# An MLP of split float32 products: matmuls in written order, weights two items ahead, sums given out by quota

## The chip, the cores and the metric

One core of one Trainium2 chip runs the whole kernel. The metric is the device time of one execution in microseconds (us), the median of several runs.

## The reference

One layer of a hybrid encoder on 256 positions (SEQ) of width 2048 (D), in float32. Ahead of the MLP stand one projection, two kinds of attention, a recurrent mixer and an output projection; the change does not touch them. The MLP is the last line:

```
D_MODEL, SEQ, D_FF = 2048, 256, 4 * 2048

def _rms_norm(x, gain):
    y = x * lax.rsqrt(jnp.mean(x * x, axis=-1, keepdims=True) + RMS_EPS)
    return y * gain

hdn = jnp.square(jax.nn.relu(_rms_norm(x, norm_mlp_pre) @ w_mlp_up))    # 256 x 8192
x = x + _rms_norm(hdn @ w_mlp_down, norm_mlp_post)                      # 256 x 2048
```

## The kernel before, in words

**A float32 product as three.** Each float32 operand is split in two parts, hi and lo, that TensorE (PE) multiplies in its faster float32 form; hi x hi, hi x lo and lo x hi are added up in PSUM. Weights come from DRAM in pieces of 128 x 1024 (512 KB) on SyncE's (SP's) DMA queue, three buffers `raw` for the up weights (L136) and six, `raw2`, for the down weights (L963). `wsplit` (L140) makes of a piece `whi`, a copy on ScalarE (ACT, L144), and `wlo`, a subtraction on VectorE (DVE, L145), three buffers of each. Activations lie as hi and lo beside each other in tiles `pk` (128 x 512).

**Entry of the MLP.** The residual `x1` is finished piece by piece on DVE (`add_mixed`, L878), turned by PE (L907, into PSUM buffers of the pool `mps`), and split into the 16 tiles `upk2` on ACT (L225) and DVE (L226). The up matmuls need these tiles one after the other.

**Items.** From there the work is a list of items, each with a `prep`, which asks for a weight piece and splits it, and a `run`, which issues the matmuls. `drive` (L939) takes them one after the other. Ahead of an item's `run` it calls the `prep` of this one and of the next one (`AHEAD` is 1), so far as that is not done. What a `run` leaves behind it goes to the list `posts` and is called right behind the next item's `run`.

- `up(q, j)` (L978) is one hidden column, 128 of the 8192 hidden units: two items of half a column. Each is one `gemm` over 8 tiles: 8 matmuls of 128 x 512 and 8 of 128 x 256 (L160, L164, L166). The column's sum lies in one of the four buffers of the PSUM pool `gps`. Its post is the evacuation: ACT copies the second half to `tmp` (L991), DVE adds the first (L992), ACT takes ReLU (L993) and square (L997).
- `forms(q, m)` (L1011) makes of two columns the seven left factors of a Strassen-like product (7 products of blocks in place of 8): sums `sfm` on DVE (L1015 to L1017), hi on ACT, lo on DVE (to L1022).
- `down(q, sb)` (L1025) is one group: the products F1 to F7 for a quarter q of the hidden units and half sb of the output columns, in four steps d. An item is one product in one step: its `prep` makes the right factor out of raw pieces, with an addition on DVE (L1033) or a DMA that accumulates (issued by GpSimd, POOL, L1036), and splits it; its `run` is 6 matmuls (L1069 to L1071). F3, F7 and F1 gather in three buffers of `gps`, F6, F2, F5 and F4 in the four of `mps`. Behind the last step (d = 3) stand the sums of the seven products into the output `y`: on DVE (L1076) and, for first ones, on ACT (L1081, L1093).

**Order of the work.** The first `drive` runs 16 columns of `up(0, ...)` with their forms. The second runs 6 groups (q = 0 to 2, sb = 0 and 1) of 4 iterations (d), 24 in all. An iteration's list (L1145) is F3, the two halves of column ua, a form, F7, F1 among them, then F6, F2, the first half of column ub, a form, F5, the second half, F4; ua and ub are the next quarter's columns. Behind the second `drive`, `tok` (L204) computes the last quarter's down product without the seven forms.

The program is written in the order of these calls. On each engine a scheduler of the framework then sets the final order, and is free to put an instruction ahead of others that were written before it. Inside `tc.manual_schedule` the engines that are named there keep the written order; an earlier stage of the kernel does this for PE (L747), the MLP does not.

Of the kernel before, what the change touches and what calls it, by code (L numbers as in the profile page):

```python
# [12 lines left out]
AF = mybir.ActivationFunctionType  # L13
ALU = mybir.AluOpType
# [6 lines left out]
AHEAD = 1  # L21
# [28 lines left out]
def hybrid_block(ctx, tc, xt, x, gains, params, consts, lora, gup, wst, out):  # L50
# [80 lines left out]
    wq = []  # L131
    side = []

    def wraw(n=None):
        raw = wpool.tile([128, HALF], F32, tag="raw", name=nm("raw"), bufs=3)
        nc.sync.dma_start(out=raw, in_=wst[wpos[0] if n is None else n])  # L136
        if n is None:
            wpos[0] += 1
        return raw
# [793 lines left out]


    AF_ = {1: 0, 2: 1, 4: 2, 7: 3, 5: 4, 6: 5, 3: 6}
    work, posts, hl = [], [], {}

    def drive():


        while work:
            prep, run = work.pop(0)
            if prep is None:
                run(None)
                continue
            for w in [(prep, run)] + [w for w in work if w[0]][:AHEAD]:
                if w not in hl:
                    hl[w] = w[0]()
            now, posts[:] = posts[:], []
            run(hl.pop((prep, run)))  # L950
            for f in now:
                f()
        while posts:
            posts.pop(0)()

    base = wst.shape[0] - 256

# [9 lines left out]
    def parts(raw):  # L967
        wsplit(raw)
        return wq.pop()
# [8 lines left out]
    def up(q, j):  # L978

        ps = [None]  # L980

        def run(hl, half):
            if half == 0:
                ps[0] = gps()
            gemm(ps[0], hl[0], hl[1], upk2[8 * half:8 * half + 8], half == 0, half == 1)
            if half:
                posts.append(post)

        def post():
            b, t = tmp(), tmp()  # L990
            A.activation(b, ps[0][:, T:2 * T], AF.Copy)  # L991
            V.tensor_tensor(t, ps[0][:, 0:T], b, ALU.add)  # L992
            A.activation(t, t, AF.Relu)  # L993
            if j % 2 == 0:
                hid[q, j // 2] = pk().bitcast(F32).rearrange("p (s t) -> p s t", s=4)
            h = hid[q, j // 2]
            A.activation(h[:, 0:4:3] if j % 2 == 0 else h[:, 1:3], t.rearrange("p (s t) -> p s t", s=2), AF.Square)  # L997
            if q == 0 and j < 8:
                A.activation(junk(), x1[j % 2][:, 512 * (j // 2):512 * (j // 2) + 512], AF.Square,
                             accum_out=ss3[:, j % 2, j // 2:j // 2 + 1])  # L1000
            if q == 0 and j in (8, 9):
                e = cpool.tile([128, 2], F32, name=nm("eps4"))
                V.tensor_reduce(e[:, 0:1], ss3[:, j % 2, :], AX.X, ALU.add)
                V.tensor_scalar(e[:, 0:1], e[:, 0:1], 1.0 / D, EPS, ALU.mult, ALU.add)
                V.tensor_tensor(e[:, 1:2], e[:, 0:1], e[:, 0:1], ALU.mult)
                V.tensor_scalar(e[:, 1:2], e[:, 1:2], EPS, None, ALU.mult)
                eps4.append(e[:, 1:2])

        return [(lambda half=half: wq.pop(0) if wq else parts(wraw(base + 64 * q + 2 * j + half)), lambda hl, half=half: run(hl, half)) for half in range(2)]

    def forms(q, m):  # L1011

        h = hid.pop((q, m))
        s = p2.tile([128, 4, 128], F32, tag="sfm", name=nm("sfm"), bufs=1)
        V.tensor_tensor(s[:, 0:2], h[:, 0:4:2], h[:, 3:4].to_broadcast([128, 2, 128]), ALU.subtract)  # L1015
        V.tensor_tensor(s[:, 2], h[:, 0], s[:, 1], ALU.add)
        V.tensor_tensor(s[:, 3], s[:, 2], h[:, 1], ALU.subtract)  # L1017
        hi, lo = fm(), fm()
        A.activation(hi[:, 0:3], h[:, 0:3], AF.Copy)
        A.activation(hi[:, 3:7], s, AF.Copy)  # L1020
        V.tensor_tensor(lo[:, 0:3], h[:, 0:3], hi[:, 0:3].bitcast(F32), ALU.subtract)
        V.tensor_tensor(lo[:, 3:7], s, hi[:, 3:7].bitcast(F32), ALU.subtract)  # L1022
        fmh[m], fml[m] = hi, lo

    def down(q, sb):  # L1025

        Q, R, vx = {}, {}, {}
        c0 = 1024 * sb
        y11, y12 = ys[0][:, c0:c0 + 512], ys[0][:, c0 + 512:c0 + 1024]
        y21, y22 = ys[1][:, c0:c0 + 512], ys[1][:, c0 + 512:c0 + 1024]  # L1030

        def add(a, b):
            V.tensor_tensor(R[a], R[a], R[b], ALU.add)  # L1033

        def dma_add(a, b):
            G.dma_start(out=R[a], in_=R[b], accum_op=ALU.add)  # L1036

        def prep(f, d):

            if f == 3:  # L1040
                R["22"], R["12"] = braw(q, c0, d, "22"), braw(q, c0, d, "12")
                r = parts(R["22"])
                add("22", "12")
            elif f == 7:
                R["11"] = braw(q, c0, d, "11")
                r = parts(R["22"])
                add("22", "11")
                dma_add("12", "11")
            elif f == 1:
                r = parts(R["11"])  # L1050
            elif f == 6:
                R["21"] = braw(q, c0, d, "21")
                r = parts(R["22"])
                dma_add("22", "21")
            elif f == 2:
                r = parts(R["21"])
            elif f == 5:
                r = parts(R["12"])
            else:
                r = parts(R["22"])  # L1060
            return r

        def run(f, d, hl):
            if d == 0:
                Q[f] = gps() if f in (3, 7, 1) else mps()
            for i in range(2):
                a, b = fmh[2 * d + i][:, AF_[f], :], fml[2 * d + i][:, AF_[f], :]
                w, wl = (x[:, 512 * i:512 * i + 512] for x in hl)
                PE.matmul(Q[f], a, w, start=d == 0 and i == 0, stop=False)  # L1069
                PE.matmul(Q[f], b, w, start=False, stop=False)  # L1070
                PE.matmul(Q[f], a, wl, start=False, stop=d == 3 and i == 1)  # L1071
            if d == 3:
                posts.append(lambda: post(f))

        def acc(y, p, op=ALU.add):
            V.tensor_tensor(y, y, p, op)  # L1076

        def first(y, p, op=ALU.add):

            if q == 0:  # L1080
                A.activation(y, p, AF.Copy, scale=1.0 if op == ALU.add else -1.0)  # L1081
            else:
                acc(y, p, op)

        def post(f):

            if f == 3:
                first(y12, Q[3], ALU.subtract)
            elif f == 1:
                first(y11, Q[1])  # L1090
            elif f == 6:
                v = vx["v"] = junk()
                A.activation(v, Q[6], AF.Copy)  # L1093
                acc(v, Q[1], ALU.subtract)
                acc(y12, v)
                acc(v, Q[7], ALU.subtract)
                first(y22, v)
            elif f == 2:
                acc(y11, Q[2])
            elif f == 5:  # L1100
                acc(y12, Q[5], ALU.subtract)
                acc(y22, Q[5], ALU.subtract)
            elif f == 4:
                first(y21, Q[4])
                acc(y21, vx["v"], ALU.subtract)

        def item(f, d):
            return (lambda: prep(f, d), lambda hl: run(f, d, hl))

        return [{f: item(f, d) for f in range(1, 8)} for d in range(4)]  # L1110

    for j in range(KT):
        work.extend(up(0, j))
        if j % 2:
            work.append((None, lambda _, m=j // 2: posts.append(lambda: forms(0, m))))
    drive()
    ys.extend(p2.tile([128, D], F32, tag="y", name=nm("y"), bufs=2) for _ in range(2))
    hp = {}
# [10 lines left out]
            hp[2 * m + i] = t  # L1129

    def later(f):
        return (None, lambda _: posts.append(f))

    def first3():
        wpos[0] = base + 3 * 64 + 32
# [4 lines left out]
    for q in range(3):  # L1140
        for sb in range(2):
            for d, F in enumerate(down(q, sb)):
                ua, ub = (up(q + 1, 8 * sb + 2 * d + j) for j in range(2))
                fs = [old.pop(0) if old else None for _ in range(2)]
                for it in (F[3], ua[0], fs[0], F[7], F[1], ua[1], F[6], F[2], ub[0], fs[1], F[5], ub[1], F[4]):  # L1145
                    if it:
                        work.append(it)
                if sb:
                    for m in (2 * d, 2 * d + 1):
                        old.append(later(lambda q=q, m=m: forms(q + 1, m) if q < 2 else split3(m)))  # L1150
    work.append((None, lambda _: first3()))
    work.extend(old)
    drive()

    hp = [hp[k] for k in range(KT)]
    g4, loads = gain(1, [pk() for _ in range(4)])
    side.extend(loads)
# [146 lines left out]
```

## Time and profile before

| | |
|---|---|
| median of 3 runs | 1560.79 us (1556.21 to 1565.39) |
| profiled execution | 1562.27 us, its span 1560.5 us |
| mean granted clock of PE | 0.991 |
| busy, share of the span | PE 98%, DVE 74%, ACT 58%, POOL 6% |
| entry and first drive | up to 951.39 us |
| second drive | 951.39 to 1462.11 us |
| last quarter, norm, output | 1462.11 to 1560.5 us |

The profile counts an engine as busy while one of its instructions runs; "PEld" is the loading of weights into PE's array, which lies beside the matmuls. In the rows of a timeline stand the start in us, the busy time in us of a run of like instructions, the engine, the line, the operation with output <- input, and in brackets the idle time ahead of it with what ended it. In the groups by line stand busy us, mean ns of one, and idle time ahead. In the rows of waits stand the total in us, the number, and the longest.

### The profile page before, as it was taken

The numbers are of one execution on the slowest core, as the hardware profiler recorded it, in microseconds if no ns is written. First come the engines' busy times: TensorE is split into PE (matmuls) and PEld (weight loads), VectorE is DVE, ScalarE is ACT, GpSimd is POOL, SyncE is SP. The second block draws the span as 40 slices with busy tenths as digits, with TensorE's granted clock in tenths as the row PEclk, the third lists the DMA queues.
The fourth block names the chain that finished last, engine by engine and source line by source line (L and its number), as shares of the span: only waits on it lengthen the run. The fifth ranks groups of instructions, "written<-read, shape, count | busy, mean of one in ns | idle before, by whom it ended". The sixth has DMA issues, their size and how long they took to land.

```text
span 1560.5 us, 22381 instructions
## 1 busy us (share of the span) xinstructions
PE 1524.2 (98%) x8318; PEld 1265.7 (81%) x8318; DVE 1157.1 (74%) x1566; ACT 907.9 (58%) x1369; POOL 88.5 (6%) x146
## 2 busy tenths in 40 slices
PE   7999999999999999999999999999999999999997
PEld 6888887887887787788887888888888877888885
DVE  7765568896558896645555778789988899888855
ACT  7565367545466554644444766567766676666542
POOL 0030001100001100000000000000000000000000
PEclk9999999999999998999999999999999999999999
DMA  7645554455445553355695557798888888887764
GB/s 242 206 159 176 162 165 150 138 190 189 135 144 179 174 164 96 125 180 188 228 306 164 171 188 201 216 266 254 242 257 250 230 236 239 263 253 232 214 200 136
DMA packets 101197, 308.50 MB, mean 198 GB/s; under 512 B 10080, under 2 KB 12512, under 8 KB 101088
## 3 DMA queue, kind: packets, MB, share of 16 engines
q1 hardware_dynamic: 91344, 280.66, 55.1%
q0 software_dynamic: 6912, 25.17, 8.7%
q8 instruction: 65, 1.06, 0.3%
q10 hardware_dynamic: 2832, 1.24, 0.3%
q14 instruction: 44, 0.36, 0.1%
HBM read 279.77 MB, written 2.10 MB: 181 GB/s over the span
## 4 chain that ended last, share of the span: by engine, by line
PE 66%; issue 10%; DVE 10%; DMA 9%; ACT 4%; POOL 0%; ACTq 0%; SPq 0%; POOLq 0%; DVEq 0%
PE gps L204 27%; PE gps L160 15%; PE gps L164 8%; DMA raw<-raw 5%; PE gps L189 5%; DVE wlo L145 5%; DMA raw<-in_wst_dram 4%; ACT whi L144 2%; PE gps L166 1%; PE mps L1069 1%; PE mps L1071 1%; PE mps L1070 1%; PE gps L1071 1%; PE gps L1069 1%; PE gps L1070 1%
## 5 line engine op out<-in xcount | busy, mean ns | idle before, releaser
L145 DVE TENSOR_TENSOR wlo<-raw,whi 128x1024 fp32r<-128x1024 f32 x590 | 716.1, 1223 | 272.4 <-ACT whi L144 254.4
L144 ACT ACTIVATE whi<-raw 128x1024 fp32r<-128x1024 f32 x590 | 618.2, 1055 | 342.0 <-PE gps L204 153.8
L160 PE MATMUL gps<-pk,whi 128*128 128x512 f32 x1501 | 386.2, 395 | 2.1 <-ACT whi L144 1.0
L160 PEld LDWEIGHTS gps<-pk,whi 128*128 128x128 f32 x1501 | 278.2, 189 | 62.4 <-issue 5.8
L204 PE MATMUL gps<-whi,pk 128*128 128x512 f32 x1144 | 293.8, 395 | 0.4 <-ACT whi L144 0.4
L204 PEld LDWEIGHTS gps<-whi,pk 128*128 128x128 f32 x1144 | 213.5, 189 | 47.0 <-issue 1.3
L164 PEld LDWEIGHTS gps<-pk,wlo 128*128 128x128 f32 x1608 | 220.1, 191 | 16.0 <-DVE wlo L145 0.7
L164 PE MATMUL gps<-pk,wlo 128*128 128x256 f32 x1608 | 225.9, 283 | 0.1
L204 PE MATMUL gps<-wlo,pk 128*128 128x512 f32 x572 | 159.8, 397 | 0.4 <-DVE wlo L145 0.4
L204 PEld LDWEIGHTS gps<-wlo,pk 128*128 128x128 f32 x572 | 107.3, 190 | 24.2 <-DVE wlo L145 1.1
L991 ACT ACTIVATE tmp<-gps 128x256 f32<-128x256 f32 x64 | 24.6, 384 | 90.7 <-PE gps L166 90.7
L1069 PE MATMUL mps<-whi,fm 128*128 128x512 f32 x192 | 76.1, 396 | 0.8 <-ACT whi L144 0.7
L1071 PE MATMUL mps<-wlo,fm 128*128 128x512 f32 x192 | 75.5, 393 | 0.4 <-DVE wlo L145 0.2
L1070 PE MATMUL mps<-whi,fm 128*128 128x512 f32 x192 | 75.0, 391 | 0.0
L1036 POOL DMA_DIRECT2D raw<-raw x48 | 41.9, 873 | 554.2 <-DVE raw L1033 313.2
L189 PE MATMUL gps<-whi,pk 128*128 128x512 f32 x264 | 71.3, 393 | 0.0
L1071 PE MATMUL gps<-wlo,fm 128*128 128x512 f32 x144 | 57.2, 397 | 2.4 <-DVE wlo L145 2.1
L1033 DVE TENSOR_TENSOR raw<-raw,raw 128x1024 f32<-128x1024 f32 x48 | 58.7, 1223 | 1.0
L189 PEld LDWEIGHTS gps<-whi,pk 128*128 128x128 f32 x264 | 49.2, 188 | 11.2 <-issue 0.7
L1069 PE MATMUL gps<-whi,fm 128*128 128x512 f32 x144 | 56.8, 395 | 1.4 <-ACT whi L144 1.4
L1070 PE MATMUL gps<-whi,fm 128*128 128x512 f32 x144 | 56.5, 392 | 0.0
L204 PE MATMUL gps<-whi,fm 128*128 128x512 f32 x208 | 51.4, 389 | 0.0
(294 smaller groups left out, 1551.7 us busy)
## 6 DMA issues: line engine op xcount, KB each, us to landing
raw<-in_wst_dram SPq DMA_DIRECT2D x518, 512.0 KB, 4.4
raw<-raw POOLq DMA_DIRECT2D x48, 512.0 KB, 6.7
x<-in_x_dram SPq DMA_DIRECT2D x8, 256.0 KB, 6.5
out_dram<-x SPq DMA_DIRECT2D x8, 256.0 KB, 2.8
x<-in_xt_dram SPq DMA_DIRECT2D x3, 512.0 KB, 7.3
fm<-in_gains_dram SPq DMA_DIRECT2D x4, 256.0 KB, 5.5
pk<-in_gains_dram SPq DMA_DIRECT2D x4, 256.0 KB, 4.5
con<-in_consts_dram SPq DMA_DIRECT2D x1, 576.0 KB, 7.8
```

Source lines behind the costliest of these rows:

```text
L144: A.activation(hi, raw, AF.Copy)
L145: V.tensor_tensor(lo, raw, hi.bitcast(F32), ALU.subtract)
L160: PE.matmul(ps, hi[:, i * 128:i * 128 + 128], pks[i], start=first and i == 0, stop=False)
L164: PE.matmul(ps[:, 0:T], lo[:, i * 128:i * 128 + 128], pks[i][:, 0:T], start=False, stop=False)
L189: PE.matmul(ps[tt], pks[k][:, c:c + 128], w[:, (k - k0) * 512:(k - k0) * 512 + 512], start=k == 0 and part == 0 and w is hl[0], stop=w is ...
L204: PE.matmul(ps[tt], pks[k][:, c:c + 128], w[:, (k - k0) * 512:(k - k0) * 512 + 512], start=k == 0 and part == 0 and w is hl[0], stop=False)
L991: A.activation(b, ps[0][:, T:2 * T], AF.Copy)
L1033: V.tensor_tensor(R[a], R[a], R[b], ALU.add)
L1036: G.dma_start(out=R[a], in_=R[b], accum_op=ALU.add)
L1069: PE.matmul(Q[f], a, w, start=d == 0 and i == 0, stop=False)
L1070: PE.matmul(Q[f], b, w, start=False, stop=False)
L1071: PE.matmul(Q[f], a, wl, start=False, stop=d == 3 and i == 1)
```

## The change

1. Both drives of the MLP stand in `tc.manual_schedule` for PE: its matmuls keep the order in which they are written.
2. `drive` prepares the next two items in place of one (`[:2]`).
3. An item has a third entry, a quota: 2, but 0 for F3, F7, F1, and the half column behind F3. The sums into `y` no longer are issued by a post as a whole but collected in the list `sums`; after each item's `run` as many of them are issued as its quota allows. `post(f)` is called at once at d = 3.
4. In an iteration the first form moves from behind ua's first half to behind its second.

```
-            for w in [(prep, run)] + [w for w in work if w[0]][:AHEAD]:
+            for w in [(prep, run, quota)] + [w for w in work if w[0]][:2]:
                 if w not in hl:
                     hl[w] = w[0]()
             now, posts[:] = posts[:], []
-            run(hl.pop((prep, run)))
-            for f in now:
+            due, sums[:] = sums[:quota], sums[quota:]
+            run(hl.pop((prep, run, quota)))
+            for f in now + due:
                 f()
-        while posts:
-            posts.pop(0)()
+        while posts or sums:
+            (posts or sums).pop(0)()
...
             if d == 3:
-                posts.append(lambda: post(f))
+                post(f)

         def acc(y, p, op=ALU.add):
-            V.tensor_tensor(y, y, p, op)
+            sums.append(lambda: V.tensor_tensor(y, y, p, op))
...
         def item(f, d):
-            return (lambda: prep(f, d), lambda hl: run(f, d, hl))
+            return (lambda: prep(f, d), lambda hl: run(f, d, hl), 0 if f in (3, 7, 1) else 2)
...
+    order = tc.manual_schedule(engines={mybir.EngineType.PE})
+    order.__enter__()
     for j in range(KT):
         work.extend(up(0, j))
...
-                for it in (F[3], ua[0], fs[0], F[7], F[1], ua[1], F[6], F[2], ub[0], fs[1], F[5], ub[1], F[4]):
+                for it in (F[3], ua[0][:2] + (0,), F[7], F[1], ua[1], fs[0], F[6], F[2], ub[0], fs[1], F[5], ub[1], F[4]):
...
     drive()

+    order.__exit__(None, None, None)
```

The first copies and the copy of Q[6] on ACT (L1081, L1093) go into `sums` in the same way. Lines behind L939 move down by one to four. Each engine has as many instructions as before, PE 6492, DVE 1524, ACT 1318; their order differs as follows.

**ACT and DVE, second step of the first group, behind column ua.** On ACT before, from F2's split (the first row) over the evacuation of ua (L991, L993, L997) and the splits for ub's first half (`whi_9061`) and F5 (`whi_9071`):

```order
L144 ACTIVATE whi_9042<-raw_9019 128x1024
L991 ACTIVATE tmp_9052<-gps_8980 128x256
L144 ACTIVATE whi_9061<-raw_9059 128x1024
L993 ACTIVATE tmp_9053<-tmp_9053 128x256
L144 ACTIVATE whi_9071<-raw_8940 128x1024
L997 ACTIVATE pk_9057<-tmp_9053 128x2x128
```

And after the change, F2's split again first, then ub's (`whi_9050`), F5's (`whi_9067`) and that of ub's second half (`whi_9079`):

```order
L144 ACTIVATE whi_9028<-raw_9015 128x1024
L144 ACTIVATE whi_9050<-raw_9048 128x1024
L992 ACTIVATE tmp_9060<-gps_8986 128x256
L144 ACTIVATE whi_9067<-raw_8926 128x1024
L144 ACTIVATE whi_9079<-raw_9077 128x1024
L994 ACTIVATE tmp_9061<-tmp_9061 128x256
```

The first copy of the evacuation stood ahead of the split for ub's first half and now stands behind it. On DVE at the same place, before (F5's split is `wlo_9072`):

```order
L145 TENSOR_TENSOR wlo_9043<-raw_9019,whi_9042 128x1024
L992 TENSOR_TENSOR tmp_9053<-gps_8980,tmp_9052 128x256
L145 TENSOR_TENSOR wlo_9062<-raw_9059,whi_9061 128x1024
L145 TENSOR_TENSOR wlo_9072<-raw_8940,whi_9071 128x1024
L145 TENSOR_TENSOR wlo_9095<-raw_9092,whi_9094 128x1024
```

And after:

```order
L145 TENSOR_TENSOR wlo_9029<-raw_9015,whi_9028 128x1024
L145 TENSOR_TENSOR wlo_9051<-raw_9048,whi_9050 128x1024
L993 TENSOR_TENSOR tmp_9061<-gps_8986,tmp_9060 128x256
L145 TENSOR_TENSOR wlo_9068<-raw_8926,whi_9067 128x1024
L145 TENSOR_TENSOR wlo_9080<-raw_9077,whi_9079 128x1024
```

The evacuation's add has changed places with the split of ub's first half, as on ACT. It does so in 47 of the second drive's 48 columns.

**PE, entry of the MLP.** Before, with `gps_7839` and `gps_7884` as the sums of the first two hidden columns, L907 the turning of the last pieces of `x1` (`x_1353`, `x_1354` are its two halves of positions):

```order
L160 MATMUL gps_7839<-pk_7750,whi_7685 128x512
L160 MATMUL gps_7884<-pk_7750,whi_7858 128x512
L907 MATMUL mps_7756<-ident,x_1353_7094 128x128 x2
L907 MATMUL mps_7756<-ident,x_1354_7095 128x128 x2
L160 MATMUL gps_7839<-pk_7753,whi_7685 128x512
L160 MATMUL gps_7839<-pk_7762,whi_7685 128x512
L160 MATMUL gps_7884<-pk_7753,whi_7858 128x512
L160 MATMUL gps_7884<-pk_7762,whi_7858 128x512
```

And after, where `gps_7847` is the first column:

```order
L160 MATMUL gps_7847<-pk_7750,whi_7685 128x512
L907 MATMUL mps_7756<-ident,x_1353_7094 128x128 x2
L907 MATMUL mps_7756<-ident,x_1354_7095 128x128 x2
L160 MATMUL gps_7847<-pk_7753,whi_7685 128x512
L160 MATMUL gps_7847<-pk_7762,whi_7685 128x512
```

The second column's matmuls no longer stand between the turnings; they follow when the first column is complete. Ahead of this place PE's rows are the same in both.

**PE, start of the third group (q = 1, sb = 0).** Before, F3 (`gps_10352`) and the first half of ua (`gps_10369`):

```order
L1069 MATMUL gps_10352<-whi_10329,fm_9771 128x512
L1070 MATMUL gps_10352<-whi_10329,fm_9772 128x512
L160 MATMUL gps_10369<-pk_7750,whi_10348 128x512
L160 MATMUL gps_10369<-pk_7753,whi_10348 128x512
L1071 MATMUL gps_10352<-wlo_10330,fm_9771 128x512
L1069 MATMUL gps_10352<-whi_10329,fm_9878 128x512
```

And after:

```order
L1070 MATMUL gps_10362<-whi_10313,fm_9831 128x512
L1071 MATMUL gps_10362<-whi_10313,fm_9832 128x512
L1072 MATMUL gps_10362<-wlo_10314,fm_9831 128x512
L1070 MATMUL gps_10362<-whi_10313,fm_9884 128x512
L1071 MATMUL gps_10362<-whi_10313,fm_9885 128x512
L1072 MATMUL gps_10362<-wlo_10314,fm_9884 128x512
L160 MATMUL gps_10373<-pk_7750,whi_10338 128x512
```

F3's six matmuls stood mixed with those of the column and now stand by themselves ahead of it; the starts of the last four groups are all mixed before and all in written order after.

More of the change, by code (lines that the diff above doesn't have):

```diff
@@ L935, in hybrid_block @@
     AF_ = {1: 0, 2: 1, 4: 2, 7: 3, 5: 4, 6: 5, 3: 6}
-    work, posts, hl = [], [], {}
+    work, posts, sums, hl = [], [], [], {}
     def drive():
         while work:
-            prep, run = work.pop(0)
+            prep, run, quota = work.pop(0)
             if prep is None:
@@ L1007, in post @@
                 eps4.append(e[:, 1:2])
-        return [(lambda half=half: wq.pop(0) if wq else parts(wraw(base + 64 * q + 2 * j + half)), lambda hl, half=half: run(hl, half)) for half in range(2)]
+        return [(lambda half=half: wq.pop(0) if wq else parts(wraw(base + 64 * q + 2 * j + half)), lambda hl, half=half: run(hl, half), 2) for half in range(2)]
     def forms(q, m):
@@ L1072, in run @@
             if d == 3:
-                posts.append(lambda: post(f))
+                post(f)
         def acc(y, p, op=ALU.add):
-            V.tensor_tensor(y, y, p, op)
+            sums.append(lambda: V.tensor_tensor(y, y, p, op))
         def first(y, p, op=ALU.add):
             if q == 0:
-                A.activation(y, p, AF.Copy, scale=1.0 if op == ALU.add else -1.0)
+                sums.append(lambda: A.activation(y, p, AF.Copy, scale=1.0 if op == ALU.add else -1.0))
             else:
@@ L1092, in post @@
                 v = vx["v"] = junk()
-                A.activation(v, Q[6], AF.Copy)
+                sums.append(lambda: A.activation(v, Q[6], AF.Copy))
                 acc(v, Q[1], ALU.subtract)
@@ L1114, in hybrid_block @@
         if j % 2:
-            work.append((None, lambda _, m=j // 2: posts.append(lambda: forms(0, m))))
+            work.append((None, lambda _, m=j // 2: posts.append(lambda: forms(0, m)), 0))
     drive()
@@ L1131, in later @@
     def later(f):
-        return (None, lambda _: posts.append(f))
+        return (None, lambda _: posts.append(f), 0)
     def first3():
@@ L1150, in hybrid_block @@
                         old.append(later(lambda q=q, m=m: forms(q + 1, m) if q < 2 else split3(m)))
-    work.append((None, lambda _: first3()))
+    work.append((None, lambda _: first3(), 0))
     work.extend(old)
     drive()
+    order.__exit__(None, None, None)
     hp = [hp[k] for k in range(KT)]
```

## The prediction

> **What bounds the kernel now.** The page first: TensorE (PE) is busy for nearly the whole span.
>
> ```profile
> span 1560.5 us, 22381 instructions
> PE 1524.2 (98%) x8318; PEld 1265.7 (81%) x8318; DVE 1157.1 (74%) x1566; ACT 907.9 (58%) x1369; POOL 88.5 (6%) x146
> ```
>
> The matmuls themselves are not changed, so time can only come from, or go into, moments in which PE issues none. The stage that the change rewrites was looked at in PE's timeline: its first and its last row, and the row behind it.
>
> ```profile
> 951.39 0.40 PE L1069 MATMUL gps<-whi,fm 128*128 128x512 f32 x1
> ...
> 1461.88 0.39 PE L1071 MATMUL mps<-wlo,fm 128*128 128x512 f32 x1
> 1462.11 0.39 PE L204 MATMUL gps<-whi,fm 128*128 128x512 f32 x1
> ```
>
> The 24 iterations of the second drive last 1462.11 - 951.39 = 510.7 us. The view by windows, one iteration a row (start and end, length, then busy time and count of PE, PEld, DVE, ACT and POOL, granted clock, DMA share, GB/s), shows what a clean one takes and which are not clean:
>
> ```profile
> 972.30:993.00 20.70, 20.70 (x108) 17.73 (x107) 16.29 (x17) 12.89 (x18) 1.39 (x2) 1.00 0.74 209
> 1118.90:1140.70 21.80, 21.43 (x108) 17.49 (x107) 20.27 (x28) 15.21 (x23) 1.74 (x2) 1.00 0.89 257
> 1204.40:1225.40 21.00, 21.00 (x108) 17.53 (x107) 18.44 (x19) 13.06 (x18) 1.74 (x2) 1.00 0.86 244
> 1246.40:1269.00 22.60, 21.56 (x108) 17.47 (x106) 20.83 (x27) 14.60 (x21) 1.74 (x2) 1.00 0.85 251
> 1290.10:1315.00 24.90, 22.81 (x112) 18.08 (x111) 24.51 (x34) 16.20 (x23) 1.74 (x2) 1.00 0.85 244
> 1377.00:1398.10 21.10, 21.10 (x107) 17.56 (x106) 17.50 (x19) 13.08 (x18) 1.74 (x2) 1.00 0.88 262
> ```
>
> A clean iteration takes 20.7 us, 24 of them 496.8 us: the stage loses 510.7 - 496.8 = 13.9 us. That is all that a better order can win there. The rows from 1118.90, 1204.40, 1290.10 and 1377.00 are the starts of the last four groups, where PE's order of before mixes the items (the rows of the order, above); they lose 1.1 + 0.3 + 4.2 + 0.4 = 6.0 us. The other 7.9 us are spread, as in the row from 1246.40, where VectorE (DVE) is busy for 20.83 of 22.6 us.
>
> **The change part by part.** Number and kind of instructions stay the same on every engine; what changes is order.
>
> (1) Entry: one column in place of two. The `up` matmuls start while the last tiles of the normed input still come, and before fills PE's waits with two columns at once, now with one. In PE's rows, at the end of that stretch, and in DVE's:
>
> ```profile
> 873.85 0.40 PE L166 MATMUL gps<-pk,whi 128*128 128x512 f32 x1
> 874.09 1.09 PE L160 MATMUL gps<-pk,whi 128*128 128x512 f32 x4
> 875.01 1.12 PE L164 MATMUL gps<-pk,wlo 128*128 128x256 f32 x8
> ```
>
> ```profile
> 867.98 0.87 DVE L226 SCALAR_TENSOR_TENSOR pk<-mps,par,pk 128x256 fp32r<-128x256 f32 x2
> 868.76 1.21 DVE L145 TENSOR_TENSOR wlo<-raw,whi 128x1024 fp32r<-128x1024 f32 x1
> 869.89 0.87 DVE L226 SCALAR_TENSOR_TENSOR pk<-mps,par,pk 128x256 fp32r<-128x256 f32 x2
> 871.30 0.48 DVE L226 SCALAR_TENSOR_TENSOR pk<-mps,par,pk 128x256 fp32r<-128x256 f32 x1 [0.54 <-ACT pk L225]
> ```
>
> At 874.09 before has two columns done. Four of the next half column's eight wide matmuls are left then, so four are done, 0.9 us of work (4 of some 0.23, 1.58 for seven below): in matmul work it had finished two columns at 874.09 - 0.9 = 873.2. After the change DVE's order has the split of 868.76 behind the last tile, and the chain DVE, ScalarE (ACT), DVE comes forward by about 0.6 us (the split's 869.89 - 868.76 = 1.13 less the 0.54 that the last step waits for ACT): the last tile is there at 871.30 + 0.48 - 0.6 = 871.2, and two matmuls finish the first column at 871.6. A column's half takes 2.77 us (979.15 to 981.92, rows below), so the second ends at 871.6 + 5.5 = 877.1. PE comes out 877.1 - 873.2 = 3.9 us behind, and it has no idle time later to catch up. I take +4.0; ends 3.0 and 4.6 (no gain in the chain).
>
> (2) Splits ahead of evacuations. With two items prepared ahead, the split of the next half column stands ahead of the evacuation of the column just done, on ACT and on DVE, in 47 of the stage's 48 columns. Only one PSUM buffer is left for columns (three of four hold F3, F7, F1), so the next column waits for that evacuation. Before, in a clean iteration, on PE, ACT and DVE:
>
> ```profile
> 979.15 1.75 PE L160 MATMUL gps<-pk,whi 128*128 128x512 f32 x7
> 980.73 1.12 PE L164 MATMUL gps<-pk,wlo 128*128 128x256 f32 x8
> 981.69 0.40 PE L166 MATMUL gps<-pk,whi 128*128 128x512 f32 x1
> 981.92 0.40 PE L1069 MATMUL mps<-whi,fm 128*128 128x512 f32 x1
> ...
> 984.66 1.98 PE L160 MATMUL gps<-pk,whi 128*128 128x512 f32 x8
> ```
>
> ```profile
> 982.12 0.38 ACT L991 ACTIVATE tmp<-gps 128x256 f32<-128x256 f32 x1 [1.93 <-PE gps L166]
> 982.40 1.05 ACT L144 ACTIVATE whi<-raw 128x1024 fp32r<-128x1024 f32 x1
> ```
>
> ```profile
> 982.53 0.42 DVE L992 TENSOR_TENSOR tmp<-gps,tmp 128x256 f32<-128x256 f32 x1 [1.07 <-ACT tmp L991]
> 983.48 1.22 DVE L145 TENSOR_TENSOR wlo<-raw,whi 128x1024 fp32r<-128x1024 f32 x1 [0.52 <-ACT whi L144]
> ```
>
> Column done, two `down` items take 981.92 to 984.66 = 2.74 us; the evacuation is over at 982.95 and the next column starts without a wait. In the new order ACT splits first: 982.12 + 1.05 = 983.17; DVE's half of the split starts 0.03 later (983.45 to 983.48 here), at 983.20. The evacuation's add then comes behind it. What a DVE step of that size takes up when another follows, what the add takes, and how PE restarts behind it, shows at the one place where the evacuation came late already:
>
> ```profile
> 1013.71 1.23 DVE L1033 TENSOR_TENSOR raw<-raw,raw 128x1024 f32<-128x1024 f32 x1
> 1014.86 0.42 DVE L992 TENSOR_TENSOR tmp<-gps,tmp 128x256 f32<-128x256 f32 x1
> ```
>
> ```profile
> 1015.42 2.08 PE L160 MATMUL gps<-pk,whi 128*128 128x512 f32 x8 [0.15 <-DVE tmp L992]
> ```
>
> 1.15 us to the next start, 0.42 for the add, 0.14 from its end (1015.28) to PE's start, and eight matmuls in 2.08 in place of 1.98. So: 983.20 + 1.15 + 0.42 + 0.14 = 984.91, against 984.66: a wait of 0.25, with the slower restart 0.35 us. There are 48 columns in the stage; at each group's end two of them (12 in all) find a buffer that F3's or F7's sum has freed and only wait for their weights. 36 x 0.35 = +12.6 us. Ends: 0 (nothing waits, as at 984.66) and, if all came as late as at 1015.42 with a split of 1.15 more ahead of the add, 36 x 1.5 = 54; I stay with 0.35, since clean iterations are the rule.
>
> [...]
>
> ```profile
> 1248.61 0.42 DVE L992 TENSOR_TENSOR tmp<-gps,tmp 128x256 f32<-128x256 f32 x1
> ```
>
> ```profile
> 1249.14 0.76 PEld L160 LDWEIGHTS gps<-pk,whi 128*128 128x128 f32 x4 [0.90 <-issue]
> ```
>
> The load starts 0.11 us after the add has ended (1249.03), not ahead of it. If it were ahead, the 0.11 and the slow restart's 0.10 would go, 36 x 0.14 = 5.0 us would stay of this term, and the sum below would be +3.0 us.
>
> (3) Written order and paced sums. The mixed group starts go: PE no longer begins an item while it holds another. The largest wait there, 1.4 us, was for weights that could not be split because two started items held the buffers:
>
> ```profile
> 1295.82 0.50 PE L1069 MATMUL gps<-whi,fm 128*128 128x512 f32 x1 [1.40 <-ACT whi L144]
> ```
>
> I give these 6.0 us back and keep the other 7.9, whose causes stay: pieces added by DMA that come late for F4's split (first row below: us, waits, longest), and sums and forms on DVE (second row: busy, mean ns). Ends: 0 and all 13.9.
>
> ```profile
> ACT whi L144 <- DMA raw<-raw: 33.3, 16, 3.5
> ```
>
> ```profile
> L1076 DVE TENSOR_TENSOR y<-y,mps 128x512 f32<-128x512 f32 x22 | 14.5, 684 | 0.0
> ```
>
> (4) Nothing for: the loads that `prep` issues, which now stand an item earlier but still wait on SP for a buffer that DVE frees (the row below); the forms moved behind ua1; the single sums, 0.68 us each (row above), which lie beside 20 us of matmuls and would cost no more than that each where a split waits behind one.
>
> ```profile
> SPq L136 <- DVE wlo L145: 811.1, 298, 11.4
> ```
>
> Sum: +4.0 + 12.6 - 6.0 = +10.6 us. The profiled execution took 1562.27 us (span 1560.5 and 1.8 around it), so it would be 1572.9. It lies 1.5 above the median of the three timed runs, 1560.79; on that the forecast is 1571.4 us.
>
> **The rivals.** 0.5% is 7.8 us, about what a measurement of this kernel can tell from no change.
>
> - The evacuation waits hide. If ACT gets to the split a quarter of a microsecond earlier than the row of 982.12 says, or F6 and F2 are late themselves, term (2) is nothing: 4.0 - 6.0 = -2.0, 1558.8 us, no change. For it: the margin is 0.25 us only. Against it: ACT can't start before PE's last matmul of the column, and the same chain stands 36 times.
> - Faster: the waits hide, and written order with weights two ahead clears the whole stage: 4.0 - 13.9 = -9.9, 1550.9 us. For it: clean iterations exist in number (20.7 at 100% PE). Against it: DVE has 20.83 of work in the iteration from 1246.40, more than 20.7.
> - Slower still: F4's weights come late (16 waits of ACT above), F3's split and the add behind it push the next column's split, and with it the evacuation, by about 1.1 us each: 10.6 + 16 x 1.1 = +28, 1589 us. For it: 1015.42 is such a place. Against it: most of these waits of ACT cost PE nothing before.
> [...]
> - That the change does not do what it says can be left out: PE's rows are in written order after it, and 47 of 48 evacuations have changed places with a split on ACT and on DVE.
>
> **How the numbers follow.** Forecast 0.50, by itself 1564 to 1580 (term 2 between 6 and 18, term 3 between -9 and -3); of it 0.39 lies over 7.8 us above the time before and 0.11 under that. Waits hidden 0.15, weights ahead 0.08 (both no change), faster 0.16, slower still 0.11. Faster by over 0.5%: 0.16. Within: 0.11 + 0.15 + 0.08 = 0.34. Slower: 0.39 + 0.11 = 0.50. The range reaches from 1552 to 1584: it takes in the two cases of no change and the nearer part of the fast and of the slow one, and leaves out the rest of these, some 0.18.
>
> **What would show it.** Right: evacuations (L992, L993 there) that start behind a split, PE's first matmul of a column waiting 0.2 to 0.3 us for `tmp` in most iterations, a clean iteration of 21.4 us in place of 20.7; the second drive beginning 4 us later; no item begun before another ends. Wrong: columns that start without a wait, iterations of 20.7 us throughout, or single waits of over a microsecond behind F4, which would make the last rival the true one.

## The result, and the profile after

The changed kernel takes 1572.94 us, the median of 7 runs (1567.50 to 1581.74), beside 1562.17 us before (7 runs, 1556.21 to 1565.39): a ratio of 1.007, 95% interval 1.0045 to 1.0096. It is slower by 10.8 us. The profiled execution took 1569.10 us, 6.8 more than the profiled one of before. The page of the changed kernel begins:

```profile
span 1567.3 us, 22411 instructions
PE 1529.3 (98%) x8318; PEld 1264.8 (81%) x8318; DVE 1153.3 (74%) x1566; ACT 915.3 (58%) x1369; POOL 86.2 (5%) x146
```

Nothing here shows the loss: the shares are those of before. It shows in PE's timeline, at the marks that part the kernel into stages: the last matmuls ahead of the entry, the start of the second drive, its end. After, then before:

```profile
849.70 0.61 PE L189 MATMUL gps<-wlo,pk 128*128 128x512 f32 x2
...
955.25 0.40 PE L1070 MATMUL gps<-whi,fm 128*128 128x512 f32 x1
...
1468.96 0.39 PE L204 MATMUL gps<-whi,fm 128*128 128x512 f32 x1
```

```profile
851.73 0.61 PE L189 MATMUL gps<-wlo,pk 128*128 128x512 f32 x2
```

The second of each pair starts 0.23 later, at 849.93 and 851.95. From there to the second drive lie 955.25 - 849.93 = 105.3 us, before 951.39 - 851.95 = 99.4: the entry and the first drive became 5.9 us longer. The second drive lasts 1468.96 - 955.25 = 513.7 us, before 510.7: 3.0 more. Behind it both have 98.4 us. The entry began 2.0 us earlier in this execution, with the same instructions ahead of it; in the profiled executions below it begins anywhere from 848.0 to 852.9. So 5.9 + 3.0 = 8.9 us belong to the change, and -2.0 is the spread of one execution: 6.9, with rounding.

The second drive by iterations, in the view by windows (columns as in the prediction): a clean one, and the counterparts of the starts and of the row that were shown of before.

```profile
998.30:1019.60 21.30, 21.29 (x108) 17.56 (x106) 14.70 (x15) 13.33 (x18) 1.70 (x2) 1.00 0.78 218
1126.36:1148.18 21.82, 21.37 (x107) 17.40 (x106) 21.25 (x29) 14.94 (x22) 1.74 (x2) 1.00 0.92 271
1212.92:1234.03 21.11, 20.98 (x108) 17.64 (x106) 18.55 (x20) 13.26 (x18) 1.92 (x3) 1.00 0.90 255
1255.33:1276.63 21.30, 21.29 (x108) 17.56 (x106) 19.76 (x26) 14.75 (x22) 1.74 (x3) 1.00 0.88 260
1297.62:1320.14 22.52, 21.33 (x108) 17.49 (x107) 22.30 (x30) 14.97 (x22) 1.74 (x2) 1.00 0.83 243
1384.22:1405.34 21.12, 20.99 (x107) 17.64 (x106) 18.66 (x20) 13.32 (x18) 2.04 (x3) 1.00 0.87 247
```

A clean iteration is 21.3 us in place of 20.7, 0.30 for each of its two columns. Two of the bad ones are better than before: 22.52 in place of 24.9 at the fifth group's start, 21.30 in place of 22.6 in the row from 1255.33. The other three starts are as long as before (21.82, 21.11 and 21.12 in place of 21.8, 21.0 and 21.1). The loss sits mostly where nothing was wrong, and the gain where much was. Note that PE is *busy* for 21.29 of 21.30 us: the record of a matmul lasts 0.39 us where one starts every 0.23, and a wait of 0.17 leaves no gap between records. The view of waits in the second drive, on PE's weight loads, finds it:

```profile
PEld gps L160 <- DVE tmp L993: 19.0, 36, 1.6
PEld gps L164 <- DVE wlo L145: 2.2, 2, 1.3
```

36 starts of columns wait for DVE's evacuation, and there is next to nothing else. Before, the same view had 15 waits for low parts, 9 for high ones, and 7 columns whose wait the profile doesn't explain ("issue"):

```profile
PEld gps L1071 <- DVE wlo L145: 6.3, 10, 1.0
PEld gps L160 <- issue: 3.8, 7, 0.9
PEld mps L1069 <- ACT whi L144: 2.8, 5, 1.1
PEld gps L1069 <- ACT whi L144: 2.6, 4, 1.8
PEld mps L1071 <- DVE wlo L145: 2.4, 5, 0.7
```

At the place that answers to 981.92 to 984.66 of before, on PE, ACT and DVE:

```profile
986.95 0.40 PE L1070 MATMUL mps<-whi,fm 128*128 128x512 f32 x1
...
989.86 2.11 PE L160 MATMUL gps<-pk,whi 128*128 128x512 f32 x8
```

```profile
987.15 1.06 ACT L144 ACTIVATE whi<-raw 128x1024 fp32r<-128x1024 f32 x1 [1.94 <-PE gps L166]
988.11 0.37 ACT L992 ACTIVATE tmp<-gps 128x256 f32<-128x256 f32 x1
```

```profile
988.24 1.23 DVE L145 TENSOR_TENSOR wlo<-raw,whi 128x1024 fp32r<-128x1024 f32 x1 [1.77 <-ACT whi L144]
989.38 0.42 DVE L993 TENSOR_TENSOR tmp<-gps,tmp 128x256 f32<-128x256 f32 x1
```

ACT's first work behind the column is the next split (987.15). Its other half takes DVE until the add can start at 989.38, which ends at 989.80; PE starts at 989.86. Two items should end 2.74 after 986.95, at 989.69: a wait of 0.17. The eight matmuls then take 2.11, 0.13 more than at 984.66 before.

The entry, on PE in the changed kernel, and the view by windows of the same stretch (the figure ahead of the DMA share is the granted clock), of after and then of before, where the entry began 2.0 us later:

```profile
866.57 0.89 PE L160 MATMUL gps<-pk,whi 128*128 128x512 f32 x2 [1.25 <-DVE pk L226]
867.99 0.89 PE L160 MATMUL gps<-pk,whi 128*128 128x512 f32 x2 [0.52 <-DVE pk L226]
868.72 1.71 PE L164 MATMUL gps<-pk,wlo 128*128 128x256 f32 x8
870.23 0.63 PE L166 MATMUL gps<-pk,whi 128*128 128x512 f32 x1
870.65 2.79 PE L160 MATMUL gps<-pk,whi 128*128 128x512 f32 x8
...
877.04 0.62 PE L160 MATMUL gps<-pk,whi 128*128 128x512 f32 x2
```

```profile
866.00:868.00 2.00, 0.90 (x3) 0.38 (x3) 1.46 (x5) 0.84 (x2) 0.00 (x0) 1.00 0.41 94
868.00:870.00 2.00, 2.00 (x9) 1.75 (x10) 0.81 (x2) 0.47 (x1) 0.00 (x0) 0.73 0.43 170
870.00:872.00 2.00, 2.00 (x8) 1.61 (x7) 0.02 (x1) 1.11 (x2) 0.00 (x0) 0.50 0.04 8
```

```profile
870.00:872.00 2.00, 2.00 (x13) 1.71 (x12) 1.25 (x3) 0.47 (x1) 0.00 (x0) 1.00 0.78 254
872.00:874.00 2.00, 2.00 (x17) 1.91 (x16) 0.42 (x1) 1.12 (x2) 0.00 (x0) 1.00 0.40 154
```

With one column only, PE waits 1.25 and 0.52 us for tiles, and behind these waits the granted clock falls to 0.50. Eight narrow matmuls start over 1.51 us (868.72 to 870.23) in place of some 0.96, and the second column takes 6.39 (870.65 to 877.04) in place of 5.5. Before, two columns filled the same time and the clock stood at 1.00.

The clock also fell once earlier in the entry, in both kernels: it is 0.50 from 858 to 860 us before, and from 856 to 862 us after. That longer fall costs little: order_second below has it too (0.50 from 858 to 864; four wide matmuls take 2.06 us at 860.75, 1.18 at 865.15), with two columns, and its entry is 0.4 us longer than before.

### The profile page after: what moved, and what is told of

Same layout as the page of the kernel before. It is cut to its first block, busy times and chain, and to the rows that moved or that the text cites. A ratio compares the mean times of both kernels' runs of the same rounds, so it can differ in the third digit from the quotient of the medians.

```text
span 1567.3 us, 22411 instructions
## 1 busy us (share of the span) xinstructions
PE 1529.3 (98%) x8318; PEld 1264.8 (81%) x8318; DVE 1153.3 (74%) x1566; ACT 915.3 (58%) x1369; POOL 86.2 (5%) x146
## 4 chain that ended last, share of the span: by engine, by line
PE 77%; issue 7%; DVE 6%; DMA 6%; ACT 3%; POOL 0%; ACTq 0%; SPq 0%; DVEq 0%; POOLq 0%
PE gps L204 27%; PE gps L160 19%; PE gps L164 10%; PE gps L189 5%; DMA raw<-in_wst_dram 3%; DMA raw<-raw 3%; DVE wlo L145 2%; PE mps L1070 2%; PE mps L1072 2%; PE mps L1071 2%; PE gps L1070 1%; PE gps L1071 1%; PE gps L1072 1%; PE gps L166 1%; ACT whi L144 1%
## 5 line engine op out<-in xcount | busy, mean ns | idle before, releaser
L160 PE MATMUL gps<-pk,whi 128*128 128x512 f32 x1501 | 391.3, 399 | 6.5 <-DVE tmp L993 3.4
L160 PEld LDWEIGHTS gps<-pk,whi 128*128 128x128 f32 x1501 | 276.8, 189 | 78.8 <-DVE tmp L993 19.0
L204 PEld LDWEIGHTS gps<-whi,fm 128*128 128x128 f32 x208 | 39.0, 188 | 8.1
```

Source lines behind the costliest of these rows:

```text
L160: PE.matmul(ps, hi[:, i * 128:i * 128 + 128], pks[i], start=first and i == 0, stop=False)
L204: PE.matmul(ps[tt], pks[k][:, c:c + 128], w[:, (k - k0) * 512:(k - k0) * 512 + 512], start=k == 0 and part == 0 and w is hl[0], stop=False)
```

## The experiments

Three of the change's four parts were undone or done alone (the moved form was not), and each suspected cost was taken away. "Entry" is the time from the last matmul ahead of it to the second drive, "drive" the second drive, both of the one profiled execution; its drive can differ by several us without a change to it (fill_entry's is 3.9 longer than the changed kernel's, evac_second's 2.6 shorter than evac_now's), so the medians and intervals decide. The kernel before, run again beside the experiments in three groups, had medians of 1562.26, 1561.48 and 1561.72 us. fill_entry stands on 2 runs and no_pace on 4, the others on 5 to 12.

| kernel | median us | ratio to before, 95% | entry | drive |
|---|---|---|---|---|
| before | 1562.17 | | 99.4 | 510.7 |
| changed | 1572.94 | 1.0070 (1.0045 to 1.0096) | 105.3 | 513.7 |
| evac_now | 1568.73 | 1.0034 (1.0022 to 1.0047) | 105.3 | 509.3 |
| one_ahead | 1568.18 | 1.0037 (1.0018 to 1.0056) | 105.2 | 515.6 |
| order_second | 1568.07 | 1.0036 (1.0023 to 1.0050) | 99.8 | 513.1 |
| order_only | 1566.71 | 1.0029 (1.0015 to 1.0043) | 105.0 | 508.6 |
| evac_now_no_sums | 1560.46 | 0.9998 (0.9979 to 1.0018) | 105.3 | 508.9 |
| evac_now_no_dma | 1554.89 | 0.9959 (0.9944 to 0.9974) | 103.9 | 499.8 |
| fill_entry | 1573.98 | 1.0081 (1.0054 to 1.0108) | 103.8 | 517.6 |
| hybrid | 1560.35 | 0.9989 (0.9973 to 1.0005) | 99.4 | 506.8 |
| evac_second | 1559.67 | 0.9991 (0.9974 to 1.0008) | 99.5 | 506.7 |
| evac_dve_add | 1553.94 | 0.9951 (0.9934 to 0.9967) | 99.5 | 503.3 |
| no_pace | 1576.12 | 1.0098 (1.0071 to 1.0125) | 105.4 | 519.8 |
| two_only | 1566.85 | 1.0036 (1.0023 to 1.0049) | 99.5 | 516.4 |

**The entry: order_second and fill_entry.** In the first, written order begins behind the first drive (`order.__enter__()` moved behind `drive()`):

```
     for j in range(KT):
         work.extend(up(0, j))
...
     drive()
+    order = tc.manual_schedule(engines={mybir.EngineType.PE})
+    order.__enter__()
```

> The changed kernel with written order on PE for the second drive only, so that the scheduler fills the entry with two columns again. Theory: the entry's delay is real and nothing later takes it up: 3.9 us less than the changed kernel, about 1569 us, the second drive beginning at 951.4. Rival: what is late later (a wait for loads or for splits) takes it up: 1573 us, no change.

The median is 4.9 us under the changed kernel's, the entry 99.8 us, the drive as long as in the changed kernel. The entry's price is real and is not taken up later. In fill_entry the first column's second half has matmuls between its own ones that fill the waits:

```
+        for i in range(7 if last else 8):
+            if last and i in (3, 5):
+                fill(5 if i == 3 else 2, hi)
```

> The changed kernel with seven more matmuls of 128 x 512 into unused buffers, five and two of them in the two waits of the first column at the entry; nothing else. In the changed kernel PE's granted clock falls to 0.50 behind these waits. Theory: the fall is part of the entry's price; with the waits filled the clock stays at 1.00 and the second column ends 1.6 us earlier: 103.7 us from the last matmul of the stage before to the second drive, where the changed kernel has 105.3 and the kernel before 99.4. Rival: the clock has to do with something else; 105.3 or, by the seven matmuls, up to 106.9.

Its windows (its entry began 2.5 us later than the changed kernel's), and the marks on PE:

```profile
870.00:872.00 2.00, 1.94 (x11) 1.30 (x10) 1.27 (x3) 0.72 (x2) 0.00 (x0) 1.00 0.58 223
872.00:874.00 2.00, 2.00 (x12) 1.67 (x11) 0.35 (x1) 1.33 (x2) 0.00 (x0) 1.00 0.04 8
874.00:877.00 3.00, 3.00 (x20) 2.67 (x19) 2.44 (x3) 1.78 (x3) 0.00 (x0) 1.00 0.37 105
```

```profile
852.15 0.61 PE L189 MATMUL gps<-wlo,pk 128*128 128x512 f32 x2
...
956.16 0.40 PE L1087 MATMUL gps<-whi,fm 128*128 128x512 f32 x1
```

The clock stays at 1.00 and the entry takes 956.16 - 852.38 = 103.8 us, 1.5 less than in the changed kernel. The whole kernel is no faster (1573.98 us), since this run's second drive came out longer; the entry alone is read here. One execution without the filling shows the same: in evac_now_no_dma PE has the same two waits (1.27 and 0.53 us), the clock happened to stay at 1.00 (1.00 in the windows from 868 to 872) and the entry took 103.9. The entries of the other six profiled executions with one column and no filling took 105.0 to 105.4. Of these, the clock is 0.50 there in the changed kernel and in evac_now (870 to 872), and in one_ahead and order_only the eight narrow matmuls behind the waits take 1.91 us, as in evac_now. So some 1.5 us of the 5.9 were the clock, and 4.4 the work that was not done in the waits. That the filling is what kept the clock up is not shown by one execution, since it stayed up once without it.

In the changed kernel the fall came behind single waits of 1.25 and 0.52 us, with PE busy for 0.90 of the 2.00 us from 866.00; in windows of 1 us the granted clock is 0.97 from 868 to 869 us and 0.50 from 869 to 872.

**The columns: evac_now.** The evacuation is called at once behind its column, not behind the next item. On ACT and DVE it stands ahead of the next split again; everything else stays.

```
             if half:
-                posts.append(post)
+                post()
```

> Theory: the second drive gains and loses in two separate places: 36 column starts wait for their evacuation behind a split (13.4 us by the rows of the changed kernel's profile), and about 11 us of other waits are gone. Here the evacuation is issued right behind its column, so that on ACT and DVE it stands ahead of that split again, and all else stays (written order, two ahead, paced sums). The 36 waits go: about 1559.5 us, 13 under the changed kernel and 2 to 3 under before; iterations of 20.7 us, the second drive at about 955. Rival: the split that then stands behind the evacuation comes late by as much and PE waits for weights instead: 1570 or more, with waits on the weights' low part at the items behind a column.

The 36 waits are gone, 13 of the 24 iterations take 20.69 us, and yet the kernel gains only 0.36%, not 0.8%. Neither theory had it whole: of 13 us some 5 came, and the waits on low parts that the rival named are there. What PE's weight loads wait for in the second drive now, and ACT there:

```profile
PEld gps L1072 <- DVE wlo L145: 8.1, 8, 1.9
PEld gps L160 <- issue: 3.2, 4, 1.3
PEld gps L164 <- DVE wlo L145: 3.1, 4, 1.2
```

```profile
ACT whi L144 <- DMA raw<-raw: 21.9, 12, 3.5
```

The low parts of weights are late again, as before the change. The place with a wait of 1.14 us on PE, and ACT ahead of it:

```profile
1208.45 0.50 PE L1072 MATMUL gps<-wlo,fm 128*128 128x512 f32 x1 [1.14 <-DVE wlo L145]
```

```profile
1203.14 2.01 ACT L144 ACTIVATE whi<-raw 128x1024 fp32r<-128x1024 f32 x2 [2.98 <-DMA raw<-raw]
```

ACT stood still for 2.98 us on F4's piece, to which a DMA still adds; the splits of the next items queue behind it, and DVE's behind those. Two runs tell that from DVE's own load.

**What is late: evac_now_no_sums and evac_now_no_dma.** Each is evac_now with one line left out: `acc` issues no sum into `y` on DVE, or `dma_add` issues no DMA.

> The kernel with the evacuation right behind its column, and the sums into y on DVE left out (66 of 72; the output is not the reference's). With the evacuation ahead of the split, some 9 us of other waits came back at the starts of groups. Theory: DVE, which has the sums beside everything else there, is what is late: without them the waits at the group starts go, 1568.7 - 8 = about 1561 us. Rival: what is late is F4's split, behind a piece that is added by DMA: 1566 or more.

(The sums on DVE are 58 by the profile's groups; the expectation miscounts them.)

> The kernel with the evacuation right behind its column, and the additions by DMA left out (the right factors of F5 and F4 lack a term; the output is not the reference's). The other side of the same question. Theory: DVE's sums are what is late, so the waits stay: 1566 us or more. Rival: F4's split behind the added piece is what is late: about 1561 us.

Without the DMA, the second drive of the profiled execution and its waits:

```profile
952.81:1452.63 499.82, 498.40 (x2546) 424.64 (x2544) 452.02 (x512) 337.69 (x469) 0.00 (x0) 1.00 0.61 198
```

```profile
PEld gps L164 <- DVE wlo L145: 2.2, 4, 1.2
PEld gps L1072 <- DVE wlo L145: 1.2, 2, 0.6
```

499.8 us, three more than 24 clean iterations, with DVE as busy as before the change (452.02 and 449.22): DVE was not too full, it was waiting. My theory falls; the median of 1554.89 lies below the rival's 1561, too. Without the sums the ratio drops too, from 1.0034 to 0.9998, but the profiled second drive hardly does (509.3 to 508.9) and ACT waits there as before; how much the sums are worth stays between 0.4 and 5.6 us. Leaving the DMA out takes away F5's addition as well as F4's, and traffic (DMA share 0.61 in place of 0.82); the next run keeps both additions and moves F4's to DVE.

**A version that is faster than both: evac_dve_add, beside evac_second.** evac_second is evac_now with written order for the second drive only. evac_dve_add changes one line more:

```
             elif f == 6:
                 R["21"] = braw(q, c0, d, "21")
                 r = parts(R["22"])
-                dma_add("22", "21")
+                add("22", "21")
```

> As the kernel just named, with F4's addition by DMA as before: the control for it. Theory: the kernel with the evacuation right behind its column, less the entry's 5.5 us: 1563 us, which is the kernel before within 0.2%. Rival: 1568 if the entry's gain is taken up by later waits.

> Written order for the second drive only, two ahead, paced sums, the evacuation right behind its column, and F4's piece added on DVE in place of by DMA (24 additions of 1.22 us on DVE; F5's stay with the DMA). Theory: it is the added piece's late landing that holds F4's split and what is queued behind it on ACT; an addition on DVE is there 1.2 us after it is issued, and DVE has room for it (16.3 of 20.7 us in a clean iteration). The stage comes to some 502 us, the kernel to about 1554, faster than both. Rival: DVE is too full at the starts of groups (20 to 24 us), the addition only moves the wait: 1560 us or more.

The second drive of evac_dve_add:

```profile
951.44:1454.77 503.33, 498.87 (x2546) 424.39 (x2544) 473.73 (x534) 338.60 (x469) 20.09 (x24) 1.00 0.75 222
```

DVE does 22 us more work than in evac_second (473.73 and 451.51) and the kernel is faster by 0.5% than before, 0.9951 (0.9934 to 0.9967), at the 1554 us that were expected, while its control is level with before. In evac_second the view of ACT's waits has the following row, 11 waits for an added piece; in evac_dve_add it has none:

```profile
ACT whi L144 <- DMA raw<-raw: 16.8, 11, 3.0
```

So F4's addition by DMA was a price, and DVE had room for it. That the price is its late landing, and not its traffic (DMA share 0.75 in place of 0.82), is likely but not proven: the loads of weights land as soon in both kernels, 4.4 and 4.3 us after issue in the median. What F5's addition by DMA costs was not tried alone.

evac_second also settles the loss itself. It takes away both the entry's price and the columns' waits and keeps the rest of the change, and at 1559.67 us (expected: 1563) it is level with the kernel before.

**Slack kept at the groups' ends only: hybrid.** Written order for the second drive, and the evacuation at once in the second and third step of a group, behind the split in the other two.

> A kernel meant to be faster than both: written order for the second drive only, two ahead, paced sums, and the evacuation right behind its column in the second and third step of a group, behind the next split (as in the change) in the last and the first. Theory: the entry's 5.5 us and half of the 36 waits (some 6 us) go, and the starts of groups keep the slack that the waits give DVE there: 1572.9 - 11.5 = about 1561 us, and down to 1557 if nothing comes late in the second and third steps. Rival: the loss only moves to other places: 1566 us, as with written order for the second drive less the evacuation's gain of 4.

1560.35 us, where 1561 was expected, but evac_second without the waits does as well (1559.67). By these medians the waits that it keeps (12 of columns, 7.2 us on the weight loads) buy what they cost, and no more.

**The parts alone: one_ahead, order_only, no_pace, two_only.** `[:AHEAD]` for `[:2]` in the changed kernel; written order in the kernel before; `post` by way of `posts` and sums at once in the changed kernel; `[:2]` in the kernel before.

> The changed kernel with the weights of one item prepared ahead, not two; written order and paced sums stay. Theory: the other 11 us were won by written order and pacing, not by the second item ahead, so the 36 waits go and nothing comes back: about 1559.5 us. Rival: two ahead is what won them; then late weights come back: 1559.5 + 11 = 1570 us, with waits for the low part at F7, F1 and F4 as before the change.

> The kernel before with written order on PE in both drives, and nothing else of the change: one ahead, sums at once. Theory: the entry costs 3.9 us, the mixed group starts go (6.0 us), no column waits: about 1560 us, the second drive beginning at 955.2. Rival: the written order by itself is what costs (PE can't fill a wait with another item): more than 1567 us.

> The changed kernel with the sums into y issued as a whole behind the next item, as before the change; written order in both drives and two ahead stay. Theory: DVE is in its written place for a moment late at the ends of groups, but the columns' waits give it room: no change, 1573 us within 3. Rival: pacing won a good part of the 11 us: 1578 us or more.

> The kernel before with two items prepared ahead and nothing else: the scheduler sets PE's order. It then puts one matmul of F5 or F3 ahead of a column's start, 0.23 us of work against the wait of 0.27. Theory: the wait needs both, two ahead and the written order; here it is all but hidden and the entry has its two columns: 1560 to 1565 us. Rival: two ahead alone costs the 36 waits: 1570 us or more.

PE's weight loads in the second drive, of one_ahead, order_only, no_pace and two_only in turn:

```profile
PEld gps L1072 <- DVE wlo L145: 12.9, 23, 1.1
```

```profile
PEld gps L1071 <- DVE wlo L145: 11.5, 15, 1.7
```

```profile
PEld gps L160 <- DVE tmp L993: 16.0, 36, 1.0
PEld gps L1072 <- DVE wlo L145: 10.2, 7, 2.3
```

```profile
PEld gps L1069 <- ACT whi L144: 7.7, 8, 1.7
PEld gps L160 <- DVE tmp L992: 6.5, 27, 0.9
```

One ahead takes the columns' waits away and brings late low parts back, 1568.2 us: the rival, and level with evac_now, so once the evacuation stands ahead of the split the second item ahead buys nothing that these runs can tell. Written order alone costs 4.5 us where -2 was expected: the entry's 5.6 and only 2.1 gained in the drive, since late weights then stop PE at the groups' starts: the last four take 91.2 us there, 88.8 before. Without pacing the weight loads wait 10.2 us for low parts, 1.1 with it, and the median is 3.2 us higher, between theory and rival. But the intervals overlap (1.0071 to 1.0125, and 1.0045 to 1.0096), so the runs don't tell the worth of pacing from nothing. The drive of 519.8, 6.1 more, overstates it: from 1310 to 1314 us the granted clock was 0.57 in that execution, by an estimate from these figures a loss of 1.7 us (0.43 of 4.0). Two ahead alone costs 5.6 us, between both expectations: the columns' waits are shorter as expected (6.5 us in place of 19.0), but the waits for F items' high parts grow (9.7 us in all, 5.4 before), which neither named; what sets them was not tried.

## Why the prediction was right, step by step

- **The bound** held: PE's work did not change (8318 matmuls in both; the record of one of 128 x 512 has a mean of 0.40 us in its faster float32 form, L160, and of 0.59 in the other, L351, before), and all of the difference is in the stages that were named.
- **Term 1, entry, +4.0: right in sign, too small.** It measured 5.9, outside its ends of 3.0 and 4.6. The step that failed is "a column's half takes 2.77 us": it took the clock at 1.00 for granted, and behind PE's waits the clock fell to 0.50. That is 1.5 us (fill_entry, and evac_now_no_dma). At a clock of 1.00 the term is 4.4, within its ends; what the last 0.4 is stays open between the chain of tiles, which was guessed at, and the earlier fall of the clock.
- **Term 2, 36 waits of 0.35, +12.6: right.** It is 36 waits and 0.30 each in a clean iteration, 10.8 us. The chain came as written, but PE starts 0.06 us behind the add, not 0.14.
- **Term 3, -6.0: right in sign, -7.8 measured** (513.7 - 496.8 - 10.8 = 6.1 us are left of the 13.9). Its reason holds in part only. The four group starts, from which the 6.0 was read, take 86.6 us in place of 88.8, and 1.2 of the 86.6 are a column's wait of 0.30 in each: 3.4 us came back there and 4.4 elsewhere, where nothing was expected. (Of the 6.0, 0.9 was no loss but work: the row of 24.90 us holds 112 matmuls, four of them the item before's.) And written order by itself did not give the starts back: it makes them longer (91.2 us in order_only), though it wins 2.1 us in the drive as a whole. The rest seems to come with pacing and with the columns' waits themselves: while PE waits 0.30 us per column, ACT and DVE catch up on late pieces. For the waits, evac_now speaks (without them the drive is 4.4 us shorter, not 10.8); how the rest divides is not shown.
- **So terms 2 and 3 are not two terms.** Taken as a sum they gave the right total; as reasons they would mislead, since undoing the waits returns 5 us and not 11 to 13 (evac_now). What I listed as a cause that stays, the piece added by DMA, is the cause that counts: with the columns' waits gone, the additions by DMA hold 9.5 us of the drive (evac_now_no_dma, F4's and F5's together).
- **Term 4, nothing** for loads and forms: no wait of PE in the changed kernel's drive names them. The paced sums, in that term too, may have been a gain of some 3 us, which the runs don't tell from nothing.
- **The rivals.** The waits don't hide: all 36 show. "Slower still" had the right mechanism at a few places, seven waits over 0.28 us, the longest 1.3, within the 6.1. "Weights ahead" (0.08 of the chances, +3.0 us) fails: no run shows a column's first weights loaded ahead of its freed buffer. In the changed kernel PE's weight loads wait for DVE's add at 36 columns; the one shown starts at 989.86, 0.06 behind the add's end.
- **The sum**: +10.6 expected, 8.9 by the terms in the profiled executions (-2.0 beside it from the spread ahead of the entry), 10.8 by medians. Term 1 was 1.9 too small, terms 2 and 3 were 1.8 too high each. One error cancels another, and what is left is made up by the medians, whose difference is 1.9 above that of the terms: that the expected 10.6 and the measured 10.8 lie so close is luck.

## What to carry to other kernels

A chain that is hidden by a quarter of a microsecond, and repeats in every iteration, can be worth more than the few long waits that catch the eye (here 36 waits of 0.30 us, 10.8 us, beside 6.0 at four groups' starts): look for what has the least room before adding something ahead of it on its engine. A wait of the bounding engine is slack for the others, so two losses read from one trace can't be added up when one is undone (here 10.8 us of waits gave 4.4 of the drive back); undo it on the chip and see what comes back. And where one late transfer holds up all that is queued behind it on an engine (ACT for 2.98 us at one place of evac_now), try to compute the operand on an engine with room, even a busy one, rather than reorder around it (evac_dve_add: 0.9951).

## What was not expected of the hardware

The granted clock of the changed kernel fell to 0.50 behind waits of 1.25 and 0.52 us, within 4 us of the first of them (0.97 from 868 to 869 us), and PE ran at that rate for 3 us (0.50 from 869 to 872). Six of the seven profiled executions with one column and no filling have the longer entry that goes with it, 105.0 to 105.4 us; in the seventh, with waits of 1.27 and 0.53 us, the clock stayed at 1.00 and the entry took 103.9. With seven matmuls of 128 x 512 for no result in the waits it stayed at 1.00 in the one execution profiled, with an entry 1.5 us shorter.
